# A hybrid attention step: one combination per tile, third buffers, and the merges' tiles beside the attention

## The chip, the cores and the metric

The kernel runs on one core of a Trainium2 chip. The metric is the device time of one execution in microseconds (us). A core has five engines that run side by side, each through its own instruction queue in order: TensorE (PE, matrix products and transposes; its weight loads are shown as PEld), VectorE (DVE), ScalarE (ACT), GpSimd (POOL) and SyncE (SP, which here only issues DMAs). Working memory is SBUF; matrix products land in PSUM, which POOL does not read in this kernel.

## The reference, cut to what matters

Two layers over 1024 latent tokens and 128 context tokens of width 1024. Each layer normalises, projects, runs three mixers side by side (A: differential attention; B: gated DeltaNet; C: mLSTM; B and C in both directions over chunks), merges their heads, projects out, and then runs a SwiGLU block. The part that is changed is the attention and the merge of B and C.

```
def diff_attention(q, k, v, lam):            # per block of 128 queries, 4 heads, two maps each
    s = einsum('bqhmd,bkhmd->bhmqk', qi, k) * scale
    p = softmax(s, axis=-1)
    w = p[:, :, 0] - lam * p[:, :, 1]
    return einsum('bhqk,bkhe->bqhe', w, v)
# merge of the heads
    a = rms_norm(a_out, attn_g) * (1.0 - lam_init)
    d = rms_norm(o_delta, delta_g) * silu(bg)
    m = sigmoid(co) * rms_norm(h_m, mlstm_g)
    mix = concatenate([a, d, m]) @ w_out
```

Latent queries see 1024 latent and 128 cached keys (1152), context queries only the 128 context keys.

## The kernel before, in words

Each layer goes through `w_in` (projections, then the preparation of the two recurrent mixers in `prep1`, `inverse` and `prep2`), `mixers` (attention, recurrence, merges and the half of the output projection that takes the recurrent mixers' outputs), the other half of the output projection, and `ffn`.

`mixers` (L979) opens a pool `attn` on the left side of SBUF and a pool `scan` on the right side. `scan` (L1000) walks over chunks of 128 tokens from both ends; every step is a `delta_step` and an `mlstm_step`, which add into the tile `OH` (all 9 chunks x 512). From step 4 on it calls `merge` (L1180) for the chunks that both directions have passed: a load of the gates into a tile `bc` (two buffers), tanh, the norm of `OH`, products, four transposes, and a store to `CAT`. All of these tiles, `OH`, `me`, `bc`, `bh`, `m2` and `ms`, live in the pool `scan`. When it closes, the pools of the next part open on the right side: `stage` (weights), `x` (24 tiles of the residual, loaded by L1449) and `cat` (inputs of the output projection, L1311). A tile that takes an address waits until the tile that had it before is done with.

`attention` (L1207) goes over 4 heads and, within a head, over pairs of query tiles: it loads `Q` (two buffers, four DMAs, L1235), and for each tile of 128 queries, for both maps: three pairs of products `s` of 128x384 (L1250) that DVE scales into `e` with a running maximum (L1251), the maximum (L1253), and one exponential of 128x1152 on ACT (L1256). Then `rz` is worked out (L1260, L1261) and the two maps are combined by w0 = w1 * rz + w0, in three groups of 384 keys: groups 0 and 1 on DVE (L1266), group 2 on POOL as a product and a sum (L1268, L1269). Each group is transposed in three (L1277) into one PSUM buffer and copied out as `wt`, groups 0 and 1 by ACT, group 2 by DVE (L1280). Nine products with `V` follow (L1284), their square and sum on ACT (L1287), the scale `z2` by two small DVE operations (L1289, L1290) and a power on POOL (L1291), the scaling into `fin` (L1292), and per pair a transpose, a scaled copy and a store (`out`, L1212 to L1218). Context tiles have one group of 128.

The order on each queue is not written out by hand: the program is traced in the order of the code, attention after the recurrence and the merges, and a planner then places each instruction by priority and by its own estimate of the times, so that attention fills in beside the recurrence, the end of `w_in` and the start of the output projection.

Of the kernel before, what the change touches and what calls it, by code (L numbers as in the profile page):

```python
# [9 lines left out]
F32 = mybir.dt.float32  # L10
F32R = mybir.dt.float32r
AF = mybir.ActivationFunctionType
ALU = mybir.AluOpType
# [4 lines left out]
P = 128  # L18
# [6 lines left out]
GW = 384  # L25
# [3 lines left out]
H = 4  # L29
EPS = 1e-6  # L30
NCH = 9
CVW = 1160
CVO = 1156
DVG = (0, 1)
DVT = (2,)
TAIL = False
WTB = 6
PLO = ()
PST = (1, 3, 5, 6)
# [31 lines left out]
class Kern:  # L71
# [907 lines left out]
    def mixers(self, l, em, src):  # L979
        with self.pool("attn") as at, self.pool("psat", PSUM) as pa:  # L980
            pz = ExitStack()
            self.at, self.pz, self.pa = at, pz.enter_context(self.pool("pssc", PSUM, "right")), pa
            att = self.attention(l)
            for _ in range(AHEAD):
                next(att)
            with self.pool("scan", side="right") as self.sc:
                self.scan(l)
            em.close()
            em, est = self.open_right()
            er, x, load = self.open_x(src)  # L990
            load(*range(NG))
            with self.pool("cat", side="right") as cp:
                for _ in att:
                    pass
                pz.close()
                with self.pool("pswo", PSUM) as pd:
                    self.w_out(l, x, 1, cp, ("ch", "cl"), pd, 12, cp)
        return em, est, er, x

    def scan(self, l):  # L1000

        nc, A, S, sc = self.nc, self.A, self.S, self.sc
        St = [sc.tile([P, 2, 2, 128], F32, name=self.nm("S")) for _ in range(2)]
        Ct = [sc.tile([P, 2, 2, 130], F32, name=self.nm("C")) for _ in range(2)]
        for t in St + Ct:
            nc.gpsimd.memset(t, 0.0)
        for d in range(2):
            for hf in range(2):
                ps = slice(64 * hf, 64 * hf + 64)
                nc.sync.dma_start(St[0][ps, d, :, 64 * hf:64 * hf + 64], A["s0"][l, d, ps])  # L1010
                nc.sync.dma_start(Ct[0][ps, d, :, 65 * hf:65 * hf + 65], A["c0"][l, d, ps])
        self.OH = sc.tile([P, NCH, 512], F32, name=self.nm("OH"))

        self.me = sc.tile([P, NCH, 2, H], F32, name=self.nm("me"))
        nc.gpsimd.memset(self.me, EPS)
        nc.vector.tensor_scalar(out=self.me[:, :, 0, :], in0=self.ss[:, :, 0:4], scalar1=64 * EPS, scalar2=64 * EPS * EPS, op0=ALU.mult, op1=ALU.add)
        for i in range(8):
            cs = (i, 7 - i)
            self.delta_step(l, cs, St[i % 2], St[(i + 1) % 2] if i < 7 else None, i > 3)
            self.mlstm_step(l, cs, Ct[i % 2], Ct[(i + 1) % 2] if i < 7 else None, i > 3)  # L1020
            if i == 3:
                so = sc.tile([P, 2, 2, 64], F32, name=self.nm("So"))
                co = sc.tile([P, 2, 2, 65], F32, name=self.nm("Co"))
                self.delta_step(l, (8, 8), None, so, False)
                self.mlstm_step(l, (8, 8), None, co, False)
                for d in range(2):
                    nc.sync.dma_start(self.O["S"][l, d], so[:, d])
                    nc.sync.dma_start(self.O["C"][l, d], co[:, d])
            if i > 4:
                for c in (i - 1, 8 - i):  # L1030
                    self.merge(l, c)
            elif i == 4:
                self.merge(l, 8)
        for c in (7, 0):
            self.merge(l, c)
# [143 lines left out]

    def merge(self, l, c):  # L1180

        nc, S, sc, pz = self.nc, self.S, self.sc, self.pz
        bc = self.t(sc, [P, 512], "bc", 2)
        nc.sync.dma_start(bc, S["BC"][c])
        th = self.t(sc, [P, 512], "bh", 2)
        nc.scalar.activation(th, bc, AF.Tanh, scale=0.5)
        hv = lambda a: a.rearrange("p (h v) -> p h v", v=64)
        src = self.OH[:, c, :]
        r = self.t(sc, [P, 512], "m2", MB)
        nc.scalar.activation(r, src, AF.Square)  # L1190
        ms = self.t(sc, [P, 8], "ms", 2)
        nc.vector.reduce_sum(ms, hv(r), axis=AX.X)
        nc.vector.scalar_tensor_tensor(out=ms, in0=ms, scalar=1.0 / 64, in1=self.me[:, c].rearrange("p a h -> p (a h)"), op0=ALU.mult, op1=ALU.add)
        nc.gpsimd.tensor_tensor(out=ms, in0=ms, in1=self.mhalf[:, :8], op=ALU.pow)
        nc.gpsimd.tensor_tensor(out=hv(r), in0=hv(src), in1=ms[:, :, None].to_broadcast([P, 8, 64]), op=ALU.mult)
        nc.vector.scalar_tensor_tensor(out=bc[:, 0:256], in0=th[:, 0:256], scalar=1.0, in1=bc[:, 0:256], op0=ALU.add, op1=ALU.mult)
        nc.gpsimd.tensor_tensor(out=r[:, 0:256], in0=r[:, 0:256], in1=bc[:, 0:256], op=ALU.mult)
        nc.vector.scalar_tensor_tensor(out=r[:, 256:512], in0=th[:, 256:512], scalar=1.0, in1=r[:, 256:512], op0=ALU.add, op1=ALU.mult)
        pt = self.ps(pz, "z", 2)
        for p in range(4):  # L1200
            nc.tensor.transpose(pt[:, 128 * p:128 * p + 128], r[:, 128 * p:128 * p + 128], self.ident)
        ct = self.t(sc, [P, 4, 128], "m2", MB)
        for i in range(2):
            nc.scalar.activation(ct[:, 2 * i:2 * i + 2], pt[:, 256 * i:256 * i + 256].rearrange("p (a t) -> p a t", a=2), AF.Copy, scale=self.hg[l][:, i:i + 1])
        nc.sync.dma_start(S["CAT"][4:8, :, 128 * c:128 * c + 128].rearrange("a p t -> p a t"), ct)

    def attention(self, l):  # L1207

        nc, S, at, pa = self.nc, self.S, self.at, self.pa
        tail = []  # L1210

        def out(fin, h, q0, nq):  # L1212
            pf = self.ps(pa, "o", 2)
# [5 lines left out]
        for h in range(H):  # L1219
# [9 lines left out]
            r0 = 64 * (h % 2)  # L1229
            for q0 in range(0, NT, 256):  # L1230
                nq = min(256, NT - q0)
                q = self.t(at, [P, 2, 2, 256], "Q", 2, F32R)
                for hh in range(2):
                    for hl in range(2):
                        nc.sync.dma_start(q[64 * hh:64 * hh + 64, :, hl, :nq].bitcast(F32),  # L1235
# [2 lines left out]
                kt = [9] if ctx else list(range(9))  # L1238
                groups = [kt] if ctx else [kt[0:3], kt[3:6], kt[6:9]]
                fin = self.t(at, [P, 256], "fin", 2)  # L1240
                for j in range(nq // 128):
# [17 lines left out]
                    rz = self.t(at, [P, 1], "rz", 4)  # L1259
                    nc.vector.reciprocal(rz, zs[1])  # L1260
                    nc.vector.scalar_tensor_tensor(out=rz, in0=rz, scalar=self.nlam, in1=zs[0], op0=ALU.mult, op1=ALU.mult)  # L1261
                    for i, ks in enumerate(groups):
                        cs = slice(GW * i, GW * i + 128 * len(ks))
                        w0, w1 = es[0][:, cs], es[1][:, cs]
                        if i in DVG:
                            nc.vector.scalar_tensor_tensor(out=w0, in0=w1, scalar=rz, in1=w0, op0=ALU.mult, op1=ALU.add)  # L1266
                            continue
                        nc.gpsimd.tensor_scalar(out=w1, in0=w1, scalar1=rz, scalar2=1.0, op0=ALU.mult, op1=ALU.mult)  # L1268
                        nc.gpsimd.tensor_tensor(out=w0, in0=w0, in1=w1, op=ALU.add)  # L1269
                    if tail and TAIL:  # L1270
                        out(*tail.pop())
                    WT = []
                    for i, ks in enumerate(groups):
                        n = len(ks)
                        p = self.ps(pa, "t", 1)
                        for a in range(n):
                            nc.tensor.transpose(p[:, 128 * a:128 * a + 128], es[0][:, GW * i + 128 * a:GW * i + 128 * a + 128], self.ident)  # L1277
                        pv = p[:, :128 * n].rearrange("p (a t) -> p a t", a=n)
                        WT.append(self.t(at, [P, 3, 128], "wt", WTB))
                        (nc.vector.tensor_copy if i in DVT else nc.scalar.copy)(WT[i][:, :n], pv)  # L1280
                    po = self.ps(pa, "o", 2)[:, :128]
                    for i, ks in enumerate(groups):
                        for a, kx in enumerate(ks):
# [2 lines left out]
                    ms = self.t(at, [P, 1], "ams", 4)  # L1286
                    nc.scalar.activation(sq, po, AF.Square, accum_out=ms)  # L1287
                    z2 = self.t(at, [P, 1], "z2", 4)
                    nc.vector.scalar_tensor_tensor(out=z2, in0=zs[0], scalar=EPS, in1=zs[0], op0=ALU.mult, op1=ALU.mult)  # L1289
                    nc.vector.scalar_tensor_tensor(out=z2, in0=ms, scalar=1.0 / 128, in1=z2, op0=ALU.mult, op1=ALU.add)  # L1290
                    nc.gpsimd.tensor_tensor(out=z2, in0=z2, in1=self.mhalf[:, 0:1], op=ALU.pow)  # L1291
                    nc.scalar.activation(fin[:, 128 * j:128 * j + 128], po, AF.Copy, scale=z2)  # L1292
                tail.append((fin, h, q0, nq))
                if not TAIL:
                    out(*tail.pop())
                yield
        if tail:
            out(*tail.pop())


    def w_out(self, l, x, half, pool, tags, psp, bufs, raw):
# [252 lines left out]
```

## Time and profile before

| | |
|---|---|
| runs, median of 3 | 3688.73 us (3680.83 to 3689.36) |
| the profiled execution, its own time | 3690.29 us |
| its span in the profile | 3688.5 us |
| granted clock of TensorE, mean | 0.969 |
| PE / PEld busy | 95% / 91% |
| DVE / ACT / POOL busy | 62% / 31% / 18% |

"Busy" is the share of the span in which an engine had an instruction running. Matrix products are pipelined and their ends are modelled, so a lone pair of products looks longer than it would in a stream. The attention of the two layers lies at about 545 to 910 us and 2375 to 2760 us of the span; the rest is projections and SwiGLU, which the change leaves as they are.

### The profile page before, as it was taken

The numbers are of one execution on the slowest core, as the hardware profiler recorded it, in microseconds if no ns is written. First come the engines' busy times: TensorE is split into PE (matmuls) and PEld (weight loads), VectorE is DVE, ScalarE is ACT, GpSimd is POOL, SyncE is SP. The second block draws the span as 40 slices with busy tenths as digits, with TensorE's granted clock in tenths as the row PEclk, the third lists the DMA queues.
The fourth block names the chain that finished last, engine by engine and source line by source line (L and its number), as shares of the span: only waits on it lengthen the run. The fifth ranks groups of instructions, "written<-read, shape, count | busy, mean of one in ns | idle before, by whom it ended". The sixth has DMA issues, their size and how long they took to land.

```text
span 3688.5 us, 59491 instructions
## 1 busy us (share of the span) xinstructions
PE 3517.3 (95%) x22770; PEld 3345.0 (91%) x22770; DVE 2296.8 (62%) x5361; ACT 1133.3 (31%) x2383; POOL 662.7 (18%) x903
## 2 busy tenths in 40 slices
PE   7999989987999999999999998999899999999998
PEld 6998888986999999999989888888788999999997
DVE  7797778887465556654486478578867243333335
ACT  6324325455241111111143341344545111111111
POOL 2014322474110000000020243035612000000001
PEclk8999988999999999999999999899999999999999
DMA  5477643864222222221132672578341111111111
GB/s 209 137 243 263 222 114 118 269 186 146 66 66 81 78 83 86 97 71 49 56 118 88 223 265 93 143 218 230 106 134 47 41 42 48 43 41 41 46 46 58
DMA packets 279011, 434.14 MB, mean 118 GB/s; under 512 B 26568, under 2 KB 188424, under 8 KB 278472
## 3 DMA queue, kind: packets, MB, share of 16 engines
q1 hardware_dynamic: 249496, 324.30, 27.6%
q10 hardware_dynamic: 29232, 106.05, 8.9%
q8 instruction: 180, 2.95, 0.3%
q14 instruction: 103, 0.84, 0.1%
HBM read 315.85 MB, written 114.39 MB: 117 GB/s over the span
## 4 chain that ended last, share of the span: by engine, by line
PE 78%; DVE 10%; DMA 5%; issue 3%; ACT 2%; POOL 1%; SPq 1%; ACTq 0%; POOLq 0%; DVEq 0%
PE pd L189 7%; PE pd L190 6%; PE pd L191 6%; PE pg L191 5%; PE pu L190 5%; PE pu L191 5%; PE pu L189 5%; PE pg L190 5%; PE pg L189 5%; PE dn L189 5%; PE dn L190 5%; PE dn L191 5%; PE s L1250 3%; PE o L1284 2%; DMA Q<-QD 1%
## 5 line engine op out<-in xcount | busy, mean ns | idle before, releaser
L362 DVE SCALAR_TENSOR_TENSOR x<-pd,mod,x 128x256 f32<-128x256 f32 (+1 forms) x832 | 404.8, 514 | 597.2 <-PE pd L191 596.0
L183 ACT CAST wh<-wr 128x1024 fp32r<-128x1024 f32 (+1 forms) x219 | 229.1, 1047 | 877.7 <-PE pu L190 462.1
L184 DVE TENSOR_TENSOR wl<-wr,wh 128x1024 fp32r<-128x1024 f32 (+1 forms) x219 | 268.7, 1233 | 169.7 <-ACT wh L183 169.2
L299 POOL TENSOR_TENSOR nacc<-nacc,nsq 128x384 f32<-128x384 f32 x48 | 51.8, 1080 | 1755.4 <-issue 1572.5
L189 PE MATMUL pd<-hh,wh 128*128 128x384 f32 x1056 | 359.4, 340 | 7.3 <-DVE x L362 5.1
L189 PE MATMUL pg<-uh,wh 128*128 128x384 f32 x1056 | 357.4, 338 | 2.6 <-ACT uh L342 2.6
L190 PE MATMUL pg<-ul,wh 128*128 128x384 f32 x1056 | 357.8, 339 | 1.0 <-DVE ul L347 1.0
L189 PE MATMUL pu<-uh,wh 128*128 128x384 f32 x1056 | 355.7, 337 | 0.0
L190 PE MATMUL pu<-ul,wh 128*128 128x384 f32 x1056 | 355.5, 337 | 0.0
L190 PE MATMUL pd<-hl,wh 128*128 128x384 f32 x1056 | 355.5, 337 | 0.0
L191 PE MATMUL pg<-uh,wl 128*128 128x384 f32 x1056 | 354.6, 339 | 0.0
L191 PE MATMUL pd<-hh,wl 128*128 128x384 f32 x1056 | 354.4, 337 | 0.0
L191 PE MATMUL pu<-uh,wl 128*128 128x384 f32 x1056 | 350.4, 336 | 0.0
L189 PE MATMUL dn<-uh,wh 128*128 128x384 f32 x864 | 296.6, 343 | 5.7 <-ACT gw L952 4.4
L190 PE MATMUL dn<-ul,wh 128*128 128x384 f32 x864 | 295.9, 342 | 0.0
L191 PE MATMUL dn<-uh,wl 128*128 128x384 f32 x864 | 295.5, 342 | 0.1
L1250 PE MATMUL s<-K,Q 128*128 128x384 f32 (+1 forms) x800 | 223.6, 388 | 30.9 <-DVE e L1251 18.1
L1251 DVE TENSOR_SCALAR_CACHE_REDUCE e<-s 128x384 f32<-128x384 f32 (+1 forms) x400 | 208.9, 540 | 33.6 <-PE s L1250 27.1
L189 PEld LDWEIGHTS pd<-hh,wh 128*128 128x128 f32 x1056 | 198.8, 188 | 18.6 <-issue 7.7
L189 PEld LDWEIGHTS pg<-uh,wh 128*128 128x128 f32 x1056 | 199.6, 189 | 4.5 <-ACT uh L342 2.8
L385 DVE TENSOR_TENSOR hs<-pu,hs 128x384 f32<-128x384 f32 x132 | 73.1, 554 | 208.5 <-PE pu L191 201.7
L191 PEld LDWEIGHTS pg<-uh,wl 128*128 128x128 f32 x1056 | 199.1, 189 | 3.8
(354 smaller groups left out, 8233.1 us busy)
## 6 DMA issues: line engine op xcount, KB each, us to landing
wr<-in_w_gu_dram ACTq DMA_DIRECT2D x88, 512.0 KB
aw<-in_w_mod_dram SPq DMA_DIRECT2D x96, 256.0 KB
wr<-in_w_dn_dram ACTq DMA_DIRECT2D x44, 512.0 KB
wr<-in_w_st_dram ACTq DMA_DIRECT2D x36, 512.0 KB
rd<-RD SPq DMA_DIRECT2D x36, 512.0 KB
aw<-in_w_mod_dram SPq DMA_DIRECT2D x32, 512.0 KB
Q<-QD SPq DMA_DIRECT2D x128, 128.0 KB
RM<-em SPq DMA_DIRECT2D x36, 384.0 KB
```

Of the source, the lines that this page charges most:

```text
L183: nc.scalar.copy(hi, r)
L184: (eng or nc.vector).tensor_tensor(out=lo, in0=r, in1=hi.bitcast(F32), op=ALU.subtract)
L189: mm(out, lhsT=wh, rhs=xh, start=start, stop=False)
L190: mm(out, lhsT=wh, rhs=xl, start=False, stop=False)
L191: mm(out, lhsT=wl, rhs=xh, start=False, stop=stop)
L299: (nc.gpsimd if k in PST else nc.vector).tensor_tensor(out=self.acc[g], in0=self.acc[g], in1=s, op=ALU.add)
L362: nc.vector.scalar_tensor_tensor(out=x[g][k][:, lo:hi], in0=ps[:, lo:hi], scalar=gate[:, k, cnd:cnd + 1], in1=x[g][k][:, lo:hi], op0=ALU.m ...
L385: nc.vector.tensor_mul(s, pu[:, :GW], s)
L1250: nc.tensor.matmul(p[:, :w], lhsT=q[:, m, hl, 128 * j:128 * j + 128], rhs=K[m][:, 128 * ks[0]:128 * ks[0] + w], start=hl == 0, stop=hl == 1)
L1251: nc.vector.tensor_scalar(out=e[:, GW * i:GW * i + w], in0=p[:, :w], scalar1=0.125, scalar2=None, op0=ALU.mult, op1=ALU.max, accum_out=mx[ ...
L1284: nc.tensor.matmul(po, lhsT=WT[i][:, a], rhs=V[:, kx, :], start=kx == kt[0], stop=kx == kt[-1])
```

## The change

The two maps are combined by one DVE operation over all 1152 keys, and POOL takes no part in it. All `wt` copies go to ACT. The two small operations of `z2` go from DVE to ACT. `Q` and `bc` get a third buffer. `OH`, `me` and the tiles of `merge` go into a pool of their own, opened after `attn` on the left side and closed together with `scan`. What was switched off before (`tail` with TAIL = False) is dropped.

```diff
-            with self.pool("scan", side="right") as self.sc:
+            with self.pool("merge") as self.mg, self.pool("scan", side="right") as self.sc:
                 self.scan(l)
...
-        self.OH = sc.tile([P, NCH, 512], F32, name=self.nm("OH"))
-        self.me = sc.tile([P, NCH, 2, H], F32, name=self.nm("me"))
+        self.OH = self.mg.tile([P, NCH, 512], F32, name=self.nm("OH"))
+        self.me = self.mg.tile([P, NCH, 2, H], F32, name=self.nm("me"))
...
     def merge(self, l, c):
-        nc, S, sc, pz = self.nc, self.S, self.sc, self.pz
-        bc = self.t(sc, [P, 512], "bc", 2)
+        nc, S, sc, pz = self.nc, self.S, self.mg, self.pz
+        bc = self.t(sc, [P, 512], "bc", 3)
...
     def attention(self, l):
-                q = self.t(at, [P, 2, 2, 256], "Q", 2, F32R)
+                q = self.t(at, [P, 2, 2, 256], "Q", 3, F32R)
...
-                    for i, ks in enumerate(groups):
-                        cs = slice(GW * i, GW * i + 128 * len(ks))
-                        w0, w1 = es[0][:, cs], es[1][:, cs]
-                        if i in DVG:
-                            nc.vector.scalar_tensor_tensor(out=w0, in0=w1, scalar=rz, in1=w0, op0=ALU.mult, op1=ALU.add)
-                            continue
-                        nc.gpsimd.tensor_scalar(out=w1, in0=w1, scalar1=rz, scalar2=1.0, op0=ALU.mult, op1=ALU.mult)
-                        nc.gpsimd.tensor_tensor(out=w0, in0=w0, in1=w1, op=ALU.add)
+                    w0, w1 = [e[:, :128 * len(kt)] for e in es]
+                    nc.vector.scalar_tensor_tensor(out=w0, in0=w1, scalar=rz, in1=w0, op0=ALU.mult, op1=ALU.add)
...
-                        (nc.vector.tensor_copy if i in DVT else nc.scalar.copy)(WT[i][:, :n], pv)
+                        nc.scalar.copy(WT[i][:, :n], pv)
...
-                    nc.vector.scalar_tensor_tensor(out=z2, in0=zs[0], scalar=EPS, in1=zs[0], op0=ALU.mult, op1=ALU.mult)
-                    nc.vector.scalar_tensor_tensor(out=z2, in0=ms, scalar=1.0 / 128, in1=z2, op0=ALU.mult, op1=ALU.add)
+                    nc.scalar.activation(z2, zs[0], AF.Square, scale=math.sqrt(EPS))
+                    nc.scalar.activation(z2, ms, AF.Identity, scale=1.0 / 128, bias=z2)
```

## Rows read from the trace of the kernel before

**Rows 1.** The page, part 1: busy us of each engine.
```profile
PE 3517.3 (95%) x22770; PEld 3345.0 (91%) x22770; DVE 2296.8 (62%) x5361; ACT 1133.3 (31%) x2383; POOL 662.7 (18%) x903
```

**Rows 2.** Stretches, layer 0: length; PE, PEld, DVE, ACT, POOL busy; clock, DMA.
```profile
560.00:637.00 77.00, 74.61 (x838) 63.89 (x837) 63.80 (x227) 45.07 (x116) 18.49 (x22) 0.90 0.35 103
637.00:820.00 183.00, 171.85 (x1344) 160.82 (x1344) 154.02 (x510) 90.75 (x208) 104.29 (x137) 0.99 0.77 228
820.00:876.00 56.00, 46.81 (x325) 39.43 (x325) 50.61 (x165) 34.89 (x84) 36.50 (x41) 1.00 0.30 83
876.00:910.00 34.00, 25.43 (x148) 21.60 (x147) 20.75 (x62) 18.98 (x48) 9.67 (x11) 0.90 0.84 276
```

**Rows 3.** The same view, stretches of layer 1.
```profile
2390.00:2440.00 50.00, 47.13 (x409) 41.54 (x409) 42.41 (x147) 26.19 (x58) 15.86 (x24) 0.92 0.50 160
2440.00:2630.00 190.00, 174.86 (x1341) 165.08 (x1341) 154.06 (x511) 90.16 (x211) 106.99 (x140) 0.96 0.71 201
2630.00:2669.00 39.00, 31.68 (x200) 26.82 (x198) 32.31 (x109) 23.07 (x56) 23.92 (x25) 0.91 0.36 97
2669.00:2760.00 91.00, 85.44 (x544) 80.65 (x543) 65.10 (x187) 42.73 (x98) 18.98 (x23) 0.98 0.46 146
```

**Rows 4.** Stretches, the products s of L1250 alone: PE busy (count), PEld busy.
```profile
560.00:637.00 77.00, 23.46 (x86) 14.92 (x85) 0.90 0.35 103
637.00:820.00 183.00, 52.89 (x196) 30.90 (x196) 0.99 0.77 228
820.00:876.00 56.00, 21.46 (x78) 12.06 (x78) 1.00 0.30 83
...
2390.00:2440.00 50.00, 19.43 (x68) 11.67 (x68) 0.92 0.50 160
2440.00:2630.00 190.00, 49.86 (x188) 30.25 (x188) 0.96 0.71 201
2630.00:2669.00 39.00, 15.10 (x54) 9.15 (x54) 0.91 0.36 97
2669.00:2760.00 91.00, 18.53 (x72) 11.97 (x70) 0.98 0.46 146
```

**Rows 5.** Timeline on PE: start us, us, engine, line, operation, count.
```profile
841.22 0.59 PE L1250 MATMUL s<-K,Q 128*128 128x384 f32 x2
...
854.00 2.51 PE L1250 MATMUL s<-K,Q 128*128 128x384 f32 x8 [0.26 <-DVE e L1251]
```

**Rows 6.** Groups by line and shape on DVE: count, busy us, mean ns, idle before.
```profile
L1266 DVE SCALAR_TENSOR_TENSOR e<-e,rz,e 128x384 f32<-128x384 f32 x128 | 105.4, 862 | 1.0
...
L724 DVE SCALAR_TENSOR_TENSOR cv<-cv,cwh,cv 128x1156 f32<-128x1156 f32 x48 | 68.2, 1420 | 0.7
...
L1280 DVE COPY wt<-t 128x384 f32<-128x384 f32 x64 | 35.2, 550 | 4.9 <-PE t L1277 4.4
...
L1289 DVE SCALAR_TENSOR_TENSOR z<-zs 128x1 f32<-128x1 f32 x72 | 19.1, 265 | 7.8 <-ACT e L1256 7.6
...
L1290 DVE SCALAR_TENSOR_TENSOR z<-ams,z 128x1 f32<-128x1 f32 x72 | 17.3, 240 | 13.3 <-ACT sq L1287 12.8
```

**Rows 7.** Line L1268 on POOL: duration ns min/median/max.
```profile
L1268 POOL TENSOR_SCALAR e<-e,rz x64: 582/890/1839, 557.7 to 2726.3; 128x384 f32<-128x384 f32 x64
```

**Rows 8.** Groups by line and shape on ACT.
```profile
L1280 ACT COPY wt<-t 128x384 f32<-128x384 f32 x128 | 60.7, 474 | 31.4 <-PE t L1277 31.2
...
L1292 ACT ACTIVATE fin<-o,z 128x128 f32<-128x128 f32 x72 | 26.4, 366 | 20.6 <-POOL z L1291 20.2
...
L152 ACT ACTIVATE le<-le 128x2 f32<-128x2 f32 x2 | 0.3, 193 | 0.0
```

**Rows 9.** Timeline of SP's DMA issues at the end of layer 0's attention.
```profile
874.43 0.55 SPq L1205 DMA_DIRECT2D CAT<-m  x1
...
876.30 20.05 SPq L1449 DMA_DIRECT2D x<-in_xT_dram  x24
```

**Rows 10.** Line L1235, who waited for its loads of Q: us, times.
```profile
  PE s L1250: 12.0, 7
```

More of the change, by code (lines that the diff above doesn't have):

```diff
@@ L33 @@
 CVO = 1156
-DVG = (0, 1)
-DVT = (2,)
-TAIL = False
 WTB = 6
@@ L1209, in attention @@
         nc, S, at, pa = self.nc, self.S, self.at, self.pa
-        tail = []
         def out(fin, h, q0, nq):
@@ L1261, in attention @@
                     nc.vector.scalar_tensor_tensor(out=rz, in0=rz, scalar=self.nlam, in1=zs[0], op0=ALU.mult, op1=ALU.mult)
-                    for i, ks in enumerate(groups):
-                        cs = slice(GW * i, GW * i + 128 * len(ks))
-                        w0, w1 = es[0][:, cs], es[1][:, cs]
-                        if i in DVG:
-                            nc.vector.scalar_tensor_tensor(out=w0, in0=w1, scalar=rz, in1=w0, op0=ALU.mult, op1=ALU.add)
-                            continue
-                        nc.gpsimd.tensor_scalar(out=w1, in0=w1, scalar1=rz, scalar2=1.0, op0=ALU.mult, op1=ALU.mult)
-                        nc.gpsimd.tensor_tensor(out=w0, in0=w0, in1=w1, op=ALU.add)
-                    if tail and TAIL:
-                        out(*tail.pop())
+                    w0, w1 = [e[:, :128 * len(kt)] for e in es]
+                    nc.vector.scalar_tensor_tensor(out=w0, in0=w1, scalar=rz, in1=w0, op0=ALU.mult, op1=ALU.add)
                     WT = []
@@ L1288, in attention @@
                     z2 = self.t(at, [P, 1], "z2", 4)
-                    nc.vector.scalar_tensor_tensor(out=z2, in0=zs[0], scalar=EPS, in1=zs[0], op0=ALU.mult, op1=ALU.mult)
-                    nc.vector.scalar_tensor_tensor(out=z2, in0=ms, scalar=1.0 / 128, in1=z2, op0=ALU.mult, op1=ALU.add)
+                    nc.scalar.activation(z2, zs[0], AF.Square, scale=math.sqrt(EPS))
+                    nc.scalar.activation(z2, ms, AF.Identity, scale=1.0 / 128, bias=z2)
                     nc.gpsimd.tensor_tensor(out=z2, in0=z2, in1=self.mhalf[:, 0:1], op=ALU.pow)
                     nc.scalar.activation(fin[:, 128 * j:128 * j + 128], po, AF.Copy, scale=z2)
-                tail.append((fin, h, q0, nq))
-                if not TAIL:
-                    out(*tail.pop())
+                out(fin, h, q0, nq)
                 yield
-        if tail:
-            out(*tail.pop())
     def w_out(self, l, x, half, pool, tags, psp, bufs, raw):
```

## The prediction

> **What bounds the kernel now.** The page comes first: over the whole span PE is busy 95%, DVE 62%, ACT 31%, POOL 18% [rows 1]. That average says that TensorE is everything, and for the projections and SwiGLU it is so; but the change touches only the attention, the merges and what opens behind them, so the view that decides is the busy time by stretch, some 350 us in layer 0 and 370 us in layer 1 [rows 2, 3]. There DVE is far above its average: 63.80 of 77 us (83%), 154.02 of 183 (84%), 50.61 of 56 (90%) in layer 0; 85%, 81%, 83% and 72% in the four stretches of layer 1. The reader is to see in the third stretch of layer 0, where the recurrence is over and merges and attention are left, that DVE at 90% is ahead of PE at 46.81 of 56 (84%).
>
> How full PE is must be read with care. A pair of products s by itself counts 0.59 us, eight in a stream take 2.51 us, so 0.31 a pair [rows 5]: about half of a lone pair's busy time is filling the pipe. The weight loads, 70% in that third stretch, 83% in the first and 88% in the second, are nearer to what PE cannot give up. By the products nearly nothing could be won in the second stretch (171.85 of 183); by the loads there are 12 points.
>
> So I take three kinds of stretch. DVE leads by 14 to 20 points over PEld in 820 to 876 and 2630 to 2669. They are level in 560 to 637 and 2390 to 2440. PE leads in 637 to 820, 2440 to 2630 and 2669 to 2760.
>
> **The change part by part.** *The combination.* A latent tile now pays on DVE two operations of 128x384 at 862 ns, one copy at 550 and the two small ones at 265 and 240 [rows 6]: 1.724 + 0.550 + 0.505 = 2.779 us. The new single operation over 1152 keys is not in the trace. The nearest row is the convolution's, the same operation on three SBUF operands of 1156 elements at 1420 ns [rows 6]. The other end is the present attention rate kept for three groups, 3 x 862 = 2.59 us. I take 1.42: the 862 is inflated, since POOL works on the third group at the same moment (its product takes 582 ns at best, 890 in the median, 1839 at worst [rows 7]), and in the new form it doesn't. Saved on DVE: 1.36 us per tile, 87 us over the 64 latent tiles; at the other end 0.19 us per tile, 12 us in all. POOL loses its two operations per tile.
>
> The spread of that POOL product, 582 to 1839 ns, shows that the two engines get in each other's way on these tiles, and the new operation stands in POOL's way for longer at a stretch; what that could cost is a rival below. The Trainium skill has a rule for it that speaks against the change (SBUF — State Buffer, Who interferes with whom): a DVE instruction with two SBUF inputs and a GpSimd instruction that reads SBUF share one port pair, and the second waits until the first is done. The trace agrees that they disturb each other; by that rule the sum would be smaller by the price of that rival, up to 21 us.
>
> *Where the saving counts.* Tiles per stretch are the s products by twelve [rows 4]: 7.2, 16.3 and 6.5 in layer 0; 5.7, 15.7, 4.5 and 6.0 in layer 1. Where DVE leads I take the whole of 1.36 us per tile, where level a half, where PE leads a quarter, since there the next thing that is late is PE itself. Whole: 11.0 tiles, 15.0 us. Half: 12.9 tiles, 8.8 us. Quarter: 38.0 tiles, 12.9 us. Sum 36.7 us. The bounds of this choice are the whole everywhere, 87 us, and nothing where PE leads or is level, 15 us.
>
> *ACT takes work over.* One more copy of 474 ns and two operations on one column, for which the nearest rows are 193 ns (128x2) and 366 ns (128x128 with a scale from a tile) [rows 8]; I take 250 each. That is 0.97 us per latent tile and 0.5 for each of the 8 context tiles, 66 us of ACT. It lies beside DVE and PE as long as ACT is not the last: ACT was at 59%, 50% and 62% in layer 0's first three stretches [rows 2]. In 820 to 876 it would be 34.89 + 6.5 x 0.97 = 41.2 us in the 47.2 that are left, 87%, with DVE at (50.61 - 8.8)/47.2 = 89%. Two engines so close with one PSUM buffer between PE's transposes and ACT's copies will not overlap in full; I charge half of the addition in the 11 tiles of this kind, 5 us. Queued behind a copy on ACT are the next exponentials, and PE's third transposes wait for the second copy. If the cover is gone everywhere, it is 66 us. The other end is that taking DVE out of the round trip of z2 (ACT to DVE to POOL to ACT) shortens it: a gain of 0.24 us per tile, 17 us in all, not counted.
>
> *First products later.* The transposes of group 0 now wait for 1.42 us instead of 0.86, but group 2 no longer waits for two POOL operations. PE has the next tile's s to do meanwhile. I take zero; the ends are 64 x 0.56 = 36 us lost and as much won.
>
> *Third buffer for Q.* PE waited 12.0 us in 7 waits for Q [rows 10]. Loads can now be issued one pair earlier; but DMA is at 0.77 in the recurrence stretch [rows 2], so they don't all come sooner. I take 4 us, between 0 and 12.
>
> *Third buffer for bc and the merges' place.* In layer 0 the 24 loads of x began 1.9 us after the last merge's store and held SP's queue for 20.05 us [rows 9], with the last tiles' stores and the loads for the output projection queued behind them. In that stretch, 876 to 910, PE is idle for 34 - 25.43 = 8.6 us. With the merges' tiles on the left side, x and the weights wait only for the recurrence's own tiles, free from about 820, the start of the third stretch, so the block moves beside the merges. I take 6 us in layer 0. In layer 1 PE had 85.44 of 91 us behind the merges, so the loads were covered: 2 us. If the moved block finds no cover, the Q and bc loads queued behind it are late: a pair of tiles in the third stretch takes 2 x 56/6.5 = 17 us, so the third Q covers all but 3 us of the 20; without it 20 us per layer would be lost. The recurrence's own tiles also change address, and its first steps wait for other predecessors. I take zero; the ends, an estimate from the first stretch, are one step of the preparation either way, about 77/8 = 10 us per layer.
>
> Sum: 36.7 - 5 + 4 + 8 = 43.7 us. The profiled execution took 3690.3 us, so 3646.6; the median of the runs is 1.6 us lower, so 3645.
>
> **The rivals.** *PE is the bound, and DVE's saving is hidden.* For it: PE at 94% and 92% in the two longest stretches. Against: PEld at 88% and 87% there, and the third stretch. Then only the 15 us of the DVE-led stretches and the 8 behind the merges come, less ACT's addition in those 11 tiles in full, 11 us: 12 us won, 3677.
>
> *All of DVE's saving comes through.* For it: DVE at 81 to 85% even where PE leads, in a queue in order, so that part of its remaining share is waiting for others. Against: PE's own work there. A half to all of 87 us with the 7 of the rest: 3639 down to 3595; I put this case at 3610.
>
> *Slower: ACT becomes the engine that is waited for.* One mechanism, at the copies wt: all three stand on ACT's queue behind exponentials, with one PSUM buffer, so PE's transposes and then DVE's next evictions wait in a ring. Its price is ACT's addition in full, 66 us, of which the 44 us otherwise won give back the greater part: 3689 + 66 - 44 = 3711. It decides from the point where ACT's share passes DVE's, which the third stretch (87 to 89%) comes close to. Against it: ACT's 50% in the long stretches.
>
> *The single operation keeps the present rate, 2.59 us.* Then DVE saves 12 us in all; at the same shares, 0.19/1.36 of 36.7, that is 5 us, with 7 of the rest: 3677. Against it stands the convolution's row.
>
> *POOL's operations of recurrence and merges wait behind the long combination.* Per layer they are 137 + 41 in the second and third stretch less three for each of 22.8 tiles [rows 2, 4], some 110. The combination covers 22.8 x 1.42 of 239 us, 13.5%; an operation that meets it waits half of 1.42 us on average, so 110 x 0.135 x 0.71 = 10.6 us per layer. The two short ones cover 16.4% with waits of 0.43: 7.8 us. If the waits are all on the path, the loss is between 6 us (the present ones were full waits too) and 21 us (they were not): at the worst 3666. For it: the spread of the POOL product. Against: DVE's mean of 862 ns beside that product is no sum of the two. This is the price of the port rule named above.
>
> **How the numbers follow.** Chances: the forecast (3625 to 3667) 0.45, and the port rival inside it 0.05; all of the saving (3595 to 3625) 0.15; hidden behind PE 0.15 and the present rate 0.05 (both 3667 to 3690); ACT's ring, or the planner's new order, slower (above 3690) 0.15. About 0.3%, 11 us, is what a measurement of this kernel tells from no change, so faster ends at 3677.7 and slower begins at 3699.8. Of the cases hidden behind PE and at the present rate half is faster: 0.50 + 0.15 + 0.10 = 0.75. Same: the other 0.10 and a little of the last, 0.13. Slower: 0.12. The range leaves out a tenth on each side: 3605 to 3700, which holds the forecast's own 3625 to 3667.
>
> **What would show it.** Right: the combination at about 1.4 us; DVE busy down by some 80 us over the span and POOL by over 100; ACT up by some 60; the merges' stretch shorter in both layers; loads of x issued before the last merge's store, and no idle 8 us of PE behind them. Wrong: the combination near 2.6 us; long waits of transposes for wt copies on ACT, and ACT near 90% in the merges' stretch; or PE's loads above 90% in the recurrence stretches with nothing won. A start of the recurrence moved by over 10 us, or a low granted clock in the attention where there was none, would be a thing that this working doesn't hold.

## The result and the profile after

The changed kernel takes 3658.88 us (median of 4 runs, 3655.34 to 3659.7) against 3688.24 us: ratio 0.9921, 95% interval 0.9906 to 0.9937, 29 us faster. The forecast was 3645 us, in a range of 3605 to 3700. The direction held, and two thirds of the 43.7 us that were summed came; the experiments show that the reasons, as they were summed, did not hold.

The page of the changed kernel, part 1:

```profile
PE 3502.0 (96%) x22770; PEld 3348.1 (92%) x22770; DVE 2230.9 (61%) x5089; ACT 1186.4 (32%) x2591; POOL 568.5 (16%) x775
```

Against [rows 1] DVE is busy 66 us less (forecast was some 80), POOL 94 us less (over 100), ACT 53 us more (some 60). The stretches of layer 0, cut at the same times as [rows 2] (length; PE, PEld, DVE, ACT, POOL busy; clock, DMA share, GB/s):

```profile
560.00:637.00 77.00, 76.10 (x835) 66.09 (x834) 58.08 (x198) 51.43 (x143) 5.76 (x11) 0.92 0.36 105
637.00:820.00 183.00, 174.46 (x1388) 167.35 (x1387) 145.00 (x466) 109.47 (x277) 86.25 (x109) 0.98 0.79 236
820.00:876.00 56.00, 46.14 (x285) 40.31 (x284) 43.58 (x129) 38.27 (x90) 25.46 (x24) 0.88 0.57 191
876.00:910.00 34.00, 33.16 (x219) 32.22 (x219) 19.21 (x48) 17.26 (x49) 2.68 (x4) 1.00 0.26 78
```

In the second stretch DVE fell from 84% to 79% and ACT rose from 50% to 60%, while the weight loads of PE rose from 88% to 91%. The fourth stretch, where PE had idled 8.6 us, is now nearly full. In the third stretch the granted clock fell from 1.00 to 0.88: a low clock where there was none, which the prediction had named as a thing that its working doesn't hold. What ACT waits for between 637 and 876 us tells which engine is now the late one (engine, line, waited for: us in total, times, longest). Before:

```profile
ACT e L1256 <- DVE nm L1253: 45.7, 25, 4.2
...
ACT wt L1280 <- PE t L1277: 5.3, 6, 1.6
```

After:

```profile
ACT wt L1269 <- PE t L1266: 23.1, 16, 3.9
...
ACT e L1253 <- DVE nm L1250: 13.5, 18, 3.0
```

The exponentials wait for DVE's maxima 13.5 us instead of 45.7; the copies wait for PE's transposes 23.1 us instead of 5.3.

Where the time went is read from two marks in each layer: the first bias sum of the late token projections, and the first Silu of SwiGLU behind the mixers. Layer 0's pair goes from 385.9 and 1038.0 us to 383.6 and 1013.9, layer 1's from 2222.5 and 2843.5 to 2199.6 and 2812.6. The distance between the two marks shrank by 21.8 us in layer 0 and by 8.0 in layer 1; the rest of the program gave 1 to 2. These marks, like every split by layer below, are of one traced execution of each kernel.

The groups on DVE, ACT and POOL that answer to [rows 6 to 8] (count, busy us, mean ns, idle before). DVE:

```profile
L1260 DVE SCALAR_TENSOR_TENSOR e<-e,rz,e 128x1152 f32<-128x1152 f32 x64 | 97.2, 1519 | 1.5
```

ACT:

```profile
L1269 ACT COPY wt<-t 128x384 f32<-128x384 f32 x192 | 91.0, 474 | 77.1 <-PE t L1266 76.2
...
L1279 ACT ACTIVATE z<-ams,z 128x1 f32<-128x1 f32 x72 | 21.3, 296 | 1.3
...
L1278 ACT ACTIVATE z<-zs 128x1 f32<-128x1 f32 x72 | 14.8, 205 | 0.6
```

The loads of x in layer 0, in the order of SP's issues, which answer to [rows 9]:

```profile
835.69 10.08 SPq L1434 DMA_DIRECT2D x<-in_xT_dram  x16
846.02 0.38 SPq L1203 DMA_DIRECT2D CAT<-m  x1
846.51 5.40 SPq L1434 DMA_DIRECT2D x<-in_xT_dram  x8
852.51 0.33 SPq L1215 DMA_DIRECT2D CAT<-ac  x1
853.92 3.26 SPq L1232 DMA_DIRECT2D Q<-QD  x4
858.24 12.19 SPq L1203 DMA_DIRECT2D CAT<-m  x2
```

They moved 41 us ahead, from 876.30 to 835.69, in among the merges' stores, as the working had it.

### The profile page after: what moved, and what is told of

It reads as the page before. It is cut to its first block, busy times and chain, and to the rows that moved or that the text cites. A ratio compares the mean times of both kernels' runs of the same rounds, so it can differ in the third digit from the quotient of the medians.

```text
span 3657.2 us, 59021 instructions
## 1 busy us (share of the span) xinstructions
PE 3502.0 (96%) x22770; PEld 3348.1 (92%) x22770; DVE 2230.9 (61%) x5089; ACT 1186.4 (32%) x2591; POOL 568.5 (16%) x775
## 4 chain that ended last, share of the span: by engine, by line
PE 82%; DVE 8%; DMA 4%; issue 2%; ACT 2%; POOL 1%; SPq 0%; ACTq 0%; POOLq 0%; DVEq 0%
PE pd L186 7%; PE pd L188 6%; PE pd L187 6%; PE pg L188 5%; PE pu L187 5%; PE pu L188 5%; PE pu L186 5%; PE pg L187 5%; PE pg L186 5%; PE dn L186 5%; PE dn L188 5%; PE dn L187 5%; PE s L1247 3%; PE o L1273 3%; PE t L1266 1%
## 5 line engine op out<-in xcount | busy, mean ns | idle before, releaser
L187 PEld LDWEIGHTS pg<-ul,wh 128*128 128x128 f32 x1056 | 199.2, 189 | 3.5 <-DVE ul L344 2.4
```

The source lines that it names most:

```text
L187: mm(out, lhsT=wh, rhs=xl, start=False, stop=False)
```

## The experiments

Each kernel below was timed beside the kernel before, whose median in these series was 3688.3 to 3689.9 us; the ratios and the us won or lost are to that kernel.

**The parts alone.** The first keeps the attention and the buffers and only moves the merges' tiles:

```diff
+            with self.pool("merge") as self.mg, self.pool("scan", side="right") as self.sc:
...
+        self.OH = self.mg.tile([P, NCH, 512], F32, name=self.nm("OH"))
+        self.me = self.mg.tile([P, NCH, 2, H], F32, name=self.nm("me"))
...
     def merge(self, l, c):
...
+        nc, S, sc, pz = self.nc, self.S, self.mg, self.pz
```

> Only the merges' tiles are placed beside the attention; attention and buffers stay as before. Theory P (the gain of 29 us comes from the place, since the loads of x and of the output projection's weights no longer wait for the last merge): 3688 less 20 to 28 us, 3660 to 3668, with the loads of x issued before the last merge's store and the first sum of the output projection in layer 0 some 20 us earlier than at 912 us. Theory D (the gain comes from DVE's relief, as the prediction summed it: 36.7 of 43.7 us): 8 us, about 3680.

3702.83 us, ratio 1.0034 (1.0023 to 1.0045): slower by 13 us. Both theories miss. SP's issues in this kernel:

```profile
847.40 7.22 SPq L1449 DMA_DIRECT2D x<-in_xT_dram  x11
854.83 0.33 SPq L1218 DMA_DIRECT2D CAT<-ac  x1
855.43 0.47 SPq L1225 DMA_DIRECT2D K<-KD  x1
856.45 0.38 SPq L1205 DMA_DIRECT2D CAT<-m  x1
856.93 0.47 SPq L1225 DMA_DIRECT2D K<-KD  x1
857.48 0.61 SPq L1235 DMA_DIRECT2D Q<-QD  x1
```

and its stretches of 10 us at that place (columns as above):

```profile
835.00:845.00 10.00, 7.33 (x47) 6.42 (x45) 8.91 (x26) 7.87 (x20) 7.74 (x9) 0.83 0.81 273
845.00:855.00 10.00, 4.22 (x32) 3.34 (x30) 6.65 (x14) 5.91 (x14) 5.05 (x5) 0.94 1.06 384
855.00:865.00 10.00, 2.50 (x8) 1.51 (x8) 1.02 (x4) 2.63 (x8) 4.17 (x4) 0.50 1.07 321
865.00:875.00 10.00, 8.19 (x23) 5.90 (x24) 5.18 (x20) 2.94 (x6) 0.00 (x0) 0.54 0.75 186
```

The reader is to see the next tiles' K and Q issued only behind the block, PE down to 4.22 and then 2.50 of 10 us, and the granted clock at 0.50 and 0.54, at or near its lower level, from 855 to 875 us. The loads of x moved as they should, and what stood behind them was starved.

The second has the attention's edits alone:

```diff
-DVT = (2,)
+DVT = ()
...
+                    w0, w1 = [e[:, :128 * len(kt)] for e in es]
+                    nc.vector.scalar_tensor_tensor(out=w0, in0=w1, scalar=rz, in1=w0, op0=ALU.mult, op1=ALU.add)
...
+                    nc.scalar.activation(z2, zs[0], AF.Square, scale=math.sqrt(EPS))
+                    nc.scalar.activation(z2, ms, AF.Identity, scale=1.0 / 128, bias=z2)
```

> Only the attention's edits (one combination, all wt copies on ACT, z2 on ACT); buffers and place stay as before. Theory D: 25 to 37 us faster, 3651 to 3663. Theory P: within 8 us of 3688; DVE's busy time falls by some 75 us all the same, and the recurrence stretch of layer 0 stays at about 196 us.

3694.15 us, ratio 1.0012 (1.0003 to 1.0021). Its DVE is busy 2227.6 us, as low as in the whole change, and the kernel is 4 us slower. Theory D, the prediction's main step taken by itself, falls.

The third has the third buffers alone (`"Q", 3` and `"bc", 3`):

> Only the third buffers of Q and bc. The prediction's 4 us for Q: about 3684. If waits for Q are filled by other work or the DMAs are the limit: no change within 5 us.

3686.68 us, ratio 0.9989 (0.9979 to 0.9999): 3 to 4 us, at the edge of what can be told. The three parts by themselves sum to +14 us; together they give -29.

The fourth is the whole change without the place:

> The whole change without the new place of the merges' tiles. Theory D: most of the gain stays, 3650 to 3665. Theory P: at most a third of it stays, 3678 to 3690, and the loads of x begin behind the last merge's store again.

3660.14 us, ratio 0.9914 (0.9897 to 0.9931): the whole gain, though x is loaded from 855.3 us, behind the last merge's store at 854.8. Theory P falls too. What the kernels that lose have in common is in one row, the reasons for idle time before the products s (us, times). It adds up PE and its weight loads, which mostly wait side by side, so it shows about twice PE's own wait. The kernel before:

```profile
  DMA Q<-QD: 19.4, 12
```

The place alone:

```profile
  DMA Q<-QD: 32.6, 15
```

The attention's edits alone:

```profile
  DMA Q<-QD: 30.7, 11
```

All but the place:

```profile
  DMA Q<-QD: 4.8, 4
```

PE by itself waited for Q 12.0 us before [rows 10], 15.3 with the place alone, 17.3 with the attention's edits alone, and 2.3 with all but the place. The third buffers alone bring it to 7.0 us, and win 3 to 4.

So a third theory, Q: either edit lets the tiles or the loads run ahead, and two buffers of Q then starve the attention; the third buffer, worth little alone, is what lets the saving through.

**The third Q with each part.** One line, `"Q", 2` to `"Q", 3`, added to the attention's edits, and to the place; and taken out of the whole change.

> The attention's edits and the third buffer of Q; bc has two buffers, the merges' tiles stay in the scan pool. Theory Q (the attention's edits speed the tiles up and are then starved for Q; the third Q lets the saving through): 3660 to 3666, nearly the whole gain of 30 us, with PE's waits for Q under 3 us per layer. Theory B (it is the third bc that lets the merges through): 3685 to 3694.

3663.73 us, ratio 0.9940 (0.9924 to 0.9955): 27 us better than the attention's edits alone by the ratios. PE by itself waits for Q 2.2 us in layer 0 and 3.7 in layer 1, about the 3 that were expected. The fourth kernel, which has three buffers of bc as well, lies 0.0026 lower, and the intervals overlap: no worth of the third bc is shown.

> The merges' tiles beside the attention and a third Q, with the attention as before. Theory Q (the place alone lost 13 us because the 24 loads of x held SP's queue while the next tiles' Q stood behind them): the loss goes, 3675 to 3688. Theory S (the planner's order of the attention behind the loads is what costs): still 3698 to 3706.

3660.30 us, ratio 0.9927 (0.9912 to 0.9942): the place goes from 13 us lost to 27 us won, with POOL still in the combination and DVE as busy as before. That is outside what theory Q expected, 3675 to 3688: the third Q does more here than take the loss back.

> The whole change with two Q buffers in place of three. Theory Q: the gain is lost, 3690 to 3710, since the place's block of loads and the faster tiles both starve for Q. Otherwise: within 8 us of 3659.

3692.86 us, ratio 1.0010 (0.9999 to 1.0021): without the third Q nothing is left of the change. PE's idle time before s in this kernel:

```profile
  DMA Q<-QD: 35.2, 13
```

And PE where the loads of x are issued, two lines without the third Q and two of the whole change:

```profile
845.00:855.00 10.00, 2.38 (x9) 1.64 (x8) 2.28 (x3) 4.54 (x14) 4.24 (x5) 0.50 1.05 381
855.00:865.00 10.00, 5.87 (x16) 3.91 (x16) 3.07 (x11) 2.38 (x5) 1.17 (x2) 0.50 0.85 208
...
845.00:855.00 10.00, 8.90 (x44) 7.86 (x44) 8.37 (x21) 4.93 (x11) 3.67 (x3) 0.66 1.06 386
855.00:865.00 10.00, 5.89 (x27) 5.07 (x26) 5.21 (x15) 5.96 (x15) 4.77 (x4) 0.73 0.44 148
```

That the third Q is the condition for the gain is shown in all three, by edits of one line. How it works is shown in part. By the two marks the third Q gives 35 us in layer 0 and nothing in layer 1 (665.7 and 609.8 us between the marks without it, 630.3 and 613.0 with it), so its worth on top of the rest is all in layer 0; on top of the attention's edits it is 14 and 9. But PE's own wait for Q falls only from 18.0 to 8.4 us, less than a third of the 33 us won. The gains don't add: the attention's edits with Q give 22 us, the place with Q 27, both 29.

**What bounds the tiles now.** To see what DVE's saving is worth, the whole change with a second combination into the dead tile:

```diff
                     nc.vector.scalar_tensor_tensor(out=w0, in0=w1, scalar=rz, in1=w0, op0=ALU.mult, op1=ALU.add)
+                    nc.vector.scalar_tensor_tensor(out=w1, in0=w1, scalar=rz, in1=w1, op0=ALU.mult, op1=ALU.add)
```

> The whole change, and on DVE behind each combination a second one of the same size into the tile that is dead by then (the output is the same): 64 x 1.5 = 97 us more of DVE. If DVE's saving is what the gain is made of, as the prediction had it at 0.27 to 1 us per us by stretch: 25 to 60 us slower than 3659. If DVE is no longer on the path at all: within 5 us of 3659.

3695.13 us, ratio 1.0020 (1.0008 to 1.0031), 36 us lost. The two operations in its profile:

```profile
L1263 DVE SCALAR_TENSOR_TENSOR e<-e,rz,e 128x1152 f32<-128x1152 f32 x64 | 94.1, 1470 | 1.0
L1264 DVE SCALAR_TENSOR_TENSOR e<-e,rz 128x1152 f32<-128x1152 f32 x64 | 92.6, 1447 | 0.3
```

36 us for 92.6 is 0.39 us per us: DVE is still partly on the path. By the marks 33 of them are lost in layer 0 and 2 in layer 1, so this mean is the price of neither layer. The addition also holds the tile e longer, so that it is no pure price of DVE.

The loads of x traced behind the attention, first with the place alone:

```diff
-            load(*range(NG))
             with self.pool("cat", side="right") as cp:
                 for _ in att:
                     pass
+                load(*range(NG))
                 pz.close()
```

> The merges' tiles beside the attention, attention and buffers as before (as in the run that took 3703 us), but the 24 loads of x are traced behind the attention instead of ahead of it, so that the planner gives the loads of Q precedence on SP's queue. Theory Q (the place alone lost time because the loads of x stood ahead of Q): the loss goes, 3670 to 3690, and PE's waits for Q fall from 32.6 us to under 20. If the memory traffic of the loads is what delays Q, wherever they stand: still 3695 or more.

3688.26 us, ratio 0.9998 (0.9986 to 1.0010): the 13 us are back. But the waits for Q are 27.4 us, not under 20, and the kernel is no faster than before: issuing the loads of x later in SP's queue takes the loss away, though that row falls by 5 us only. What the third Q adds to the place isn't explained by it.

> The whole change, and the loads of x traced behind the attention. PE's remaining waits for Q in the whole change are 12.0 us over both layers; if they are due to the loads of x, 3647 to 3655, faster than the change; if the third Q covers all that matters, within 4 us of 3659.

3655.27 us, ratio 0.9912 (0.9896 to 0.9928). The row of waits for Q falls from 12.0 to 7.0 us, but the interval overlaps that of the change; no difference is shown.

The third group's copy back on DVE (`nc.vector.tensor_copy if i in (2,)`):

> The whole change with the copy of the third group's wt back on DVE. It takes 64 x 0.47 = 30 us from ACT and gives DVE 64 x 0.55 = 35 us. At the 0.37 us per us that twice the combination showed for DVE, 13 us slower, 3672. If ACT is the engine waited for after the change (the rival's ring), 5 to 20 us faster than 3659.

3651.67 us, ratio 0.9903 (0.9886 to 0.9921): the 13 us slower that the price of DVE gave are out. By the median it is 7 us faster than the change, inside the 5 to 20 us of the other expectation, but the intervals overlap; whether the copy is cheaper on DVE is not shown.

Last, three of the nine products with V:

```diff
+                            if len(kt) == 1 or a == 0:
                                 nc.tensor.matmul(po, lhsT=WT[i][:, a], rhs=V[:, kx, :], ...)
```

> The whole change, but of the nine products with V per latent tile only three are made (one of each group; the attention's result is incomplete): 64 x 6 products of 0.12 us, 46 us less of TensorE. If TensorE is what the attention is bound by now: 25 to 46 us faster than 3659. If the chain through DVE and ACT sets the tiles' pace: under 12 us faster.

3625.67 us, ratio 0.9823 (0.9802 to 0.9845), 36 us faster than the change by the ratios. It falls in TensorE's interval, but on a wrong premise: each product with V is two instructions here, so the page has 22002 instead of 22770 products, 768 less, and their row falls from 174.3 us busy to 86.0, by 88 us. That is 0.4 us per us, as much as DVE. By the marks 5 of these us are won in layer 0 and 28 in layer 1, the other way round than with DVE's second operation. So far as one trace of each kernel tells, after the change layer 1 answers to TensorE's work and not to DVE's, and layer 0 answers to DVE's; what TensorE is worth in layer 0 is hidden by the lower clock shown in the last section.

## Why the prediction was right, and where it was not

*The combination's price* held: 1519 ns against 1420, so DVE pays 2.779 - 1.519 = 1.26 us less per tile instead of 1.36. The rival of the present rate (2.59 us) is out.

*ACT's addition* held: 205 + 296 ns for the two operations of z2 against 2 x 250, 474 for the copy. The rival of ACT's ring, 3711, is out: ACT's copies wait for PE, as the rows above show. Whether ACT's copies cost a few us is open: a copy taken from ACT gave 7 us by the medians, with overlapping intervals.

*Where the saving counts* is the step that failed, with the assumption under it that the terms add. The 31.7 us that the attention's edits were to bring (36.7 less 5) came to a loss of 4 us when they stood alone and 22 with a third Q. The stretches' shares of DVE did say that DVE was ahead; they did not say that with two buffers of Q none of the saving comes through.

*The third Q* is the term that was mis-sized: 4 us, with 12 as its upper end, since PE waited 12.0 us for Q before [rows 10]. On top of the rest it is worth 33 us (ratio 1.0010 against 0.9921). A wait of the profile before doesn't bound what its removal gives in a kernel whose tiles come faster: without the third Q the same wait, PE's own, is 18.0 us there, and even that is about half of the 33. The clock, which stands at 0.50 from 845 to 865 us without the third Q, may be a part of the rest; no run takes it apart.

*The merges' place* did what it was to do, but nothing that can be told is won by it on top of the rest (0.9914 without it, 0.9921 with it); the sum had 8 us. The working had its risk right: 20 us per layer lost if the moved block finds no cover, with the third Q as the cover. Alone, it lost 13 us, all of it in layer 0 by the marks.

*By layer*, the sum had, split by its tiles, 24 us for layer 0 and 19 for layer 1; they gave 21.8 and 8.0. In layer 1 the last store of the attention came 534.5 us behind the first mark before and 536.8 after: with the place the output projection's first sum starts at 2638.4 instead of 2708.3 us, and its products take PE ahead of the attention's last tiles. Without the place layer 1 gave 16.8 us (2204.1 to 2808.3), layer 0 19.8. That the order on PE's queue is the reason is read from these marks and was not tried by itself.

*The port rival.* POOL lost two operations that took 72 + 52 us, and yet is busy only 94 us less. The same sum into OH that had 732 ns in the median and 912 at most has these durations now (min/median/max):

```profile
L1176 POOL TENSOR_TENSOR OH<-OH,s x18: 725/734/1845, 747.4 to 2580.6; 128x256 f32<-128x256 f32 x18
```

1845 less 734 is 1.1 us, most of a combination. One of the long ones beside its combination (start us, us):

```profile
746.67 1.82 DVE L1260 SCALAR_TENSOR_TENSOR e<-e,rz,e 128x1152 f32<-128x1152 f32 x1
747.36 1.72 POOL L1176 TENSOR_TENSOR OH<-OH,s 128x256 f32<-128x256 f32 x1
```

The sum starts inside the combination and ends 0.59 us behind its end at 748.49, so some of POOL's operations do wait for it. The Trainium skill's rule (SBUF — State Buffer, Who interferes with whom) is borne out by these rows. What it costs in time no run here takes apart.

So the forecast came near by a sum that was too large on two terms and too small on one. That these errors fell against each other was luck: with the third Q at the 4 us of the sum, the other terms as measured would have given nothing.

Of the kernels run that compute everything, three have ratios below the change's 0.9921: the loads behind the attention (0.9912), the third copy on DVE (0.9903), and all but the place (0.9914). None is shown to be faster than the change.

What stays open: why the place with a third Q gives 27 us while DVE is as busy as before, and why the three parts together stop at about 30. A third Q also lets the planner place the instructions in another order; no run kept the order and changed the buffer alone, so that rival of the waits for Q is untested. That DVE's work counts in layer 0 and hardly in layer 1 speaks against one bound for both; no run changed the buffers of e or of the transposes.

## What to carry to other kernels

Where engines take turns on few buffers, price edits in pairs with the buffer that feeds them: a third buffer that gives 3 us alone can be the condition for 30. Before a block of loads is moved ahead on an in-order queue, name what will stand behind it there, and give that one more buffer first. A wait in the profile of before is no upper bound on what its cure is worth together with a speedup.

## What the runs showed of the hardware that was not expected

A short starvation of TensorE costs more than its idle time: in the run with the place alone PE was at 4.22 of 10 us from 845 to 855 us and at 2.50 from 855 to 865, and the granted clock stood at 0.54, nearly all of it the lower level of 1.2 GHz, for the next 10 us though PE was busy again for 8.19 of them.

With two thirds of the products with V left out, the clock stayed at that level through the attention's first 90 us, in which it rises at 568 to 593 us in the traces of the other kernels. Stretches of that run:

```profile
545.00:570.00 25.00, 23.82 (x197) 19.20 (x195) 16.09 (x56) 14.69 (x40) 0.00 (x0) 0.50 0.70 199
570.00:600.00 30.00, 30.00 (x207) 24.90 (x203) 16.84 (x56) 15.18 (x41) 1.12 (x2) 0.50 0.19 62
600.00:637.00 37.00, 36.52 (x283) 30.86 (x282) 22.92 (x73) 20.45 (x56) 2.53 (x2) 0.50 0.20 65
```

and of the whole change:

```profile
545.00:570.00 25.00, 25.00 (x183) 20.73 (x181) 15.97 (x52) 12.80 (x33) 0.00 (x0) 0.50 0.55 149
570.00:600.00 30.00, 29.33 (x344) 25.75 (x343) 22.58 (x78) 21.83 (x61) 1.68 (x3) 0.95 0.27 85
600.00:637.00 37.00, 36.77 (x422) 31.91 (x423) 30.11 (x104) 25.14 (x72) 4.08 (x8) 1.00 0.48 135
```

Both show PE busy nearly throughout at a different clock, so part of what is left out of TensorE's work can be lost again to a lower clock, and the 0.4 us per us above holds that in it. It isn't so in every execution: three of the four runs, the traced one among them, took 3624 to 3629 us at a mean clock of 0.959 or 0.960, the fourth 3609.93 us at 0.967.
